# A transformer-mixer layer: memory queries and keys of all heads move into the seven-product stage

## The chip, the cores and the metric

The kernel runs on one core of a Trainium2 chip. The metric is device time in microseconds (us) of one execution, smaller is better. TensorE (PE) does the matrix products; VectorE (DVE) and ScalarE (ACT) read and write the tiles beside it; GpSimd (POOL) and SyncE (SP) mostly issue DMA transfers.

## The reference

One layer works on T = 640 tokens (512 latent, 128 context) of width 1024. Around it lie two half-step feed-forwards; between them stands the token mixer, which this change is about:

```
mq, mk, mv, mo, mg, dq, dk, dv, gm, gd = split_cols(h @ w_in)
dq, dk = rmsnorm(dq), rmsnorm(dk)            # 8 attention heads, 2 x 64 wide
q_att, keys = rope_2d(dq), rope_2d(dk)       # latent tokens only, + cached keys
s   = einsum('bqhcd,bkhcd->bhcqk', q_att, keys) * scale
pr  = softmax(s);  w = pr[:, :, 0] - lam * pr[:, :, 1]
att = rmsnorm(einsum('bhqk,bkhv->bqhv', w, vals)) * (1 - lam_init)
h_f = mlstm_chunkwise(mq / 16, mk, mv, log_i[0], log_f[0])   # 4 heads, 256 wide,
h_b = mlstm_chunkwise(reversed the same)                     # chunks of 128 tokens
hm  = rmsnorm(h_f + h_b) * sigmoid(mo)
y   = sigmoid(gm) * (hm @ w_br_m) + sigmoid(gd) * (att @ w_br_d)
out = y @ w_out
```

So ten projections of the same normalised activations h feed an attention branch and a memory branch (an mLSTM scan in both directions). mq, mk, mv, mo are 4 heads each; each head's 1024 x 256 block of weights is called a granule here, as is each quarter of the gates gm and gd and each pair of attention heads' dq, dk or dv. Nine vectors of modulation, products of a conditioning vector with columns of w_ada, scale, shift and gate the three parts.

## The kernel before, in words

Matrices are in float32, split into a high and a low part, and a product is three matmuls (high-high, high-low, low-high); a chunk of 128 of the inner dimension (8 chunks) thus gives 24 matmuls for one output tile, a *unit*. The mixer has four parts in time.

*The seven-product stage* (class `Gates`, a `Winograd`). For a granule whose output lies feature by feature, a 2 x 2 split of both operands needs 7 half-size products in place of 8: 7 x 4 x 3 = 84 matmuls of 128x320 (tile `ps_f`) rather than 96. VectorE and ScalarE make the sums of weights (`ww`, `wB`, `wC`) and combine the results, which go to DRAM (`g_out`, then `mq_dram`, `mk_dram`, `o_dram`, `gm_dram`, `gd_dram`). `self.work` is the list of granules in order: six of the gates, query and key of memory head 0, four of `mo`. A table `IN_GATES` places modulation tiles (class `Columns`, two VectorE passes `junk<-raw_a,csil` for each) at its granules.

*Attention.* Nine fill units, then eight heads. Each head has five slots, qi = 0 to 4, one for each 128 queries. A slot's scores (`sc`, 8 matmuls) are followed on VectorE by a reduce (`mn<-sc`, 1536 wide), on ScalarE by two exponentials (`p<-sc,mn`), on VectorE by `rc`, `r` and the mix `p`, on TensorE by the transposes `ps_wT` of slot qi, on ScalarE by the copies `wT`, and then by the values (`ps_o`). At the end of a head come its norm, the packing of the next head's queries and keys (`qT`, `kH`, `kL`) and the copy `aT`.

*The fill queue* (`fill`). Projections which are not due yet are units in one queue: token granules (`ps_t`, 5 units of 24 matmuls 128x256, results by token) and feature granules (`ps_p`, 4 units of 24 matmuls 128x320). The code calls `fill.units(n)` between the parts of a slot; the table `UNITS` tells how many stand at the two places of each slot of each head. A granule needs its weights loaded (`raw`), and split by ScalarE (`wH`) and VectorE (`wL`). A token granule of attention queries or keys is followed by norm and rope work on VectorE: `ss` (1280 wide), a scaling `*ry`, a multiplication by `g_kn` or `g_qn` and three passes 1024 wide with `ropeA` and `ropeB`.

*The memory scan* (class `Memory`). For each memory head, P (decays), va (values) and C (state) are loaded on SP's queue; ten cells (5 chunks x 2 directions) run; `fill.slot` places fill units there by a rate set with `fill.pace`. After the last cell the fill queue is drained, and the units of the next product follow (`w_brd`), interleaved with the last norm (`finish`).

Before the change queries and keys of memory heads 1 to 3 are feature granules of the fill queue; head 0's are read back from DRAM in attention head 1. Order on VectorE, ScalarE and TensorE is partly that of a scheduler and partly the order written out by hand (`with written()`).

Of the kernel before, what the change touches and what calls it, by code (L numbers as in the profile page):

```python
# [7 lines left out]
F32 = mybir.dt.float32  # L8
# [12 lines left out]
T = NS + NP  # L21
# [10 lines left out]
def tile_trunk(ctx: ExitStack, tc: tile.TileContext, a: dict):  # L32
# [1432 lines left out]
    def rope_place(of):  # L1465
        if not in_pools:
            return rope_p[0].tile([128, 5, 256], F32, tag="pk", name="rope", bufs=2)
        return pair(of, 2, "rope").rearrange("p a b -> p (a b)").rearrange("p (t n) -> p t n", t=5)

    at_rope = [None]  # L1470

# [24 lines left out]

    def project_q(pr, now=lambda f: f()):
        def make():
            q_tok[pr] = t = qk.tile([128, 5, 256], F32, tag="qtok", name="q_tok")

            def evac(p, i):
                act(t[:, i, :], p, AF.Copy)
                if i == 4:
                    now(lambda: qk_norm_rope(t, tabs[0]))

            return evac

        return a["w_dq"][pr], make

    def project_k(pr, now=lambda f: f()):  # L1510
        def make():
            if pr % 2:
                t = pair("k", 3, "k_tok").rearrange("p a b -> p (a b)").rearrange("p (t n) -> p t n", t=5)
            else:
                t = qk.tile([128, 5, 256], F32, tag="ktok", name="k_tok")
# [12 lines left out]

        return a["w_dk"][pr], make

    def project_v(pr):
        def make():
            v_tok[pr] = t = ap.tile([128, 7, 256], F32, tag="vtok", name="v_tok")
            nc.sync.dma_start(out=t[:, 4:6, :], in_=a["cache_v"][:, :, pr * 256 : (pr + 1) * 256])

            def evac(p, i):
                act(t[:, i if i < 4 else 6, :], p, AF.Copy)
                if i == 4:
                    nc.sync.dma_start(out=a["new_v"][:, pr * 256 : (pr + 1) * 256], in_=t[:, 6, :])

            return evac

        return a["w_dv"][pr], make
# [144 lines left out]
    def begin_pools():  # L1688
        gates.close()
        in_pools["k"] = ctx.enter_context(tc.tile_pool(name="mlk", bufs=1, side="right"))  # L1690
        in_pools["q"] = queries_of.enter_context(tc.tile_pool(name="mlq", bufs=1, side="right"))

    queries_of = ExitStack()

# [11 lines left out]

    mqT, mkT = {}, {}

    def q_evac(h):
        mqT[h] = pair("q", h, "mqT")  # L1710
        return lambda p, mt, hf: act(mqT[h][:, mt, half(hf)], p, AF.Copy, scale=0.0625)

    def load_memory(h):
        for box, tag, src in ((mqT, "q", mq_dram), (mkT, "k", mk_dram)):
            box[h] = pair(tag, h, f"m{tag}T")
            nc.sync.dma_start(out=box[h], in_=src[:, 2 * h : 2 * h + 2, :])

    def k_evac(h, by_act=False):
        mkT[h] = pair("k", h, "mkT")
        if by_act:  # L1720
            return lambda p, mt, hf: act(mkT[h][:, mt, half(hf)], p, AF.Copy)
        return lambda p, mt, hf: vec.tensor_copy(mkT[h][:, mt, half(hf)], p)

    def v_evac(h):
        def f(p, i):
# [12 lines left out]
    def values_of(h):  # L1738
        token((a["w_mv"][h], lambda: v_evac(h)))

    def queries_of_memory(h):
        feature(a["w_mq"][h], lambda: q_evac(h))

    def keys_of_memory(h, **kw):
        feature(a["w_mk"][h], lambda: k_evac(h, **kw))

    def projections(pr):
        token(project_k(pr))
        token(project_q(pr))
# [35 lines left out]
    class Gates(Winograd):  # L1785
# [3 lines left out]
        def __init__(self, fp, tmp, psum):  # L1789
            self.fp, self.tmp, self.psum = fp, tmp, psum  # L1790
            self.part = {(kh, hf): Of(kh, hf) for kh in range(2) for hf in range(2)}
            gate = [(a[n], dst, g, self.plain) for g in range(3) for n, dst in (("w_gd", gd_dram), ("w_gm", gm_dram))]
            rest = [(a["w_mq"], mq_dram, 0, self.query), (a["w_mk"], mk_dram, 0, self.plain)]
# [152 lines left out]
    def aside(hd, qi, part):  # L1946
# [8 lines left out]
        if part == 0 and hd == 1 and qi in (2, 3):  # L1955
            gate_cols()

    two, one = (1, 1), (1, 0)
    UNITS = {
        0: (two, two, two, two, one, (1, 1, 1)), 1: (two, two, two, one, one, (0,)),  # L1960
        2: (one,) * 5 + ((1, 1, 1),), 3: (two, one, one, one, one, (0,)),
        4: (one,) * 5 + ((1, 1, 1),), 5: (two, one, one, one, one, (1,)),
        6: (two, one, one, one, one, (1, 1, 1)), 7: (two, one, one, one, (0, 0), (0, 0)),
    }
    late = None
    for hd in range(8):
        H = heads[hd]
        odd = hd % 2
        for qi in range(5):
            n = UNITS[hd][qi]  # L1970
            with written():
                H.scores(qi)
                if qi > 0:
                    H.turn(qi - 1)
                H.soft(qi)
            aside(hd, qi, 0)
            fill.units(n[0])
            with written():
                H.mix(qi)
            if late is not None:  # L1980
                late()
                late = None
            if qi > 0:
                with written():
                    H.values(qi - 1)
            if qi == 3 and hd < 7:
                with written():
                    heads[hd + 1].pack()
            aside(hd, qi, 1)
            if (hd, qi) == (0, 2):  # L1990
                begin_pools()
            elif (hd, qi) == (1, 0):
                load_memory(0)
            fill.units(n[1])
            with written():
                fill.ahead()
        n = UNITS[hd][-1]
        with written():
            H.turn(4)
        if hd < 7:  # L2000
            N = heads[hd + 1]
            N.queries()
            fill.units(n[0])
            with written():
                H.values(4)
            H.finish_norm()
            if odd:
                for i in range(5):
                    fill.one()
                    if i in (0, 1):  # L2010
                        N.keys(i)
                    if i == 1:
                        with written():
                            fill.ahead()
            else:
                N.keys(0)
                fill.units(n[1])
                N.keys(1)
                with written():
                    fill.ahead()  # L2020
                fill.units(n[2])
# [174 lines left out]
    for h in range(4):  # L2196
# [372 lines left out]
```

## Time and profile before

| | us |
|---|---|
| median of 3 runs (lowest, highest) | 1813.63 (1813.38, 1814.05) |
| profiled execution | 1812.29 |
| its span, first to last instruction | 1810.5 |
| seven-product stage | 504.0 to 652.3 |
| attention, first fill units | 652.3 to 680.8 |
| attention, heads 0 to 7 | 680.8 to 1074.7 |
| memory scan and its drain | 1074.7 to about 1218 |

The profile gives each engine's busy time; since TensorE's matmul ends are modelled, the time from one issue to the next tells more than a busy share. "Idle before" names what ended an engine's wait. A chain of work, followed back from the last instruction, tells which engine the time belongs to. L75 is the line of the matmul helper, L51 that of ScalarE's helper, L54 and L57 those of VectorE's: groups are told apart by their tiles.

### The profile page before, as it was taken

How to read it: one execution, taken by the hardware profiler on the slowest of the kernel's cores; microseconds unless marked ns; L12 is line 12 of the kernel's file. 1: busy time of each engine (PE TensorE's matmuls, PEld its weight loads, DVE VectorE, ACT ScalarE, POOL GpSimd, SP SyncE). 2: the span in 40 equal slices, each digit the busy share in tenths (PEclk: the TensorE clock that was granted, in tenths of full speed). 3: DMA queues.
4: the chain of work that ended last, by engine and by line, in shares of the span. 5: the costliest groups of instructions: out<-in, count | busy, mean ns of one | idle time of the engine just before them, and what ended most of it. 6: DMA issues, size and time to landing. Idle time of an engine off the chain costs nothing.

```text
span 1810.5 us, 30758 instructions
## 1 busy us (share of the span) xinstructions
PE 1784.8 (99%) x12550; PEld 1743.7 (96%) x12550; DVE 1345.2 (74%) x2162; ACT 899.6 (50%) x1579; POOL 41.0 (2%) x72
## 2 busy tenths in 40 slices
PE   8999999999999999999999999999999999999998
PEld 7999999999999999999999998899999999999998
DVE  6889987677888765858585547877668888897485
ACT  5654544333655455656565546562326545554432
POOL 0000000100000000000000000000000000000010
PEclk9999999999999999999999999999999999999999
DMA  8355566977245544221221134565652455557992
GB/s 327 111 198 177 185 232 224 349 227 266 84 139 182 194 143 131 78 70 63 69 69 60 64 106 129 181 248 209 216 173 78 134 174 185 203 179 274 352 310 84
DMA packets 132207, 311.36 MB, mean 172 GB/s; under 512 B 10017, under 2 KB 93217, under 8 KB 119009
## 3 DMA queue, kind: packets, MB, share of 16 engines
q1 hardware_dynamic: 120690, 263.64, 42.2%
q0 software_dynamic: 10688, 43.13, 7.4%
q8 instruction: 98, 1.61, 0.4%
q10 hardware_dynamic: 688, 2.63, 0.4%
q14 instruction: 43, 0.35, 0.1%
HBM read 240.49 MB, written 68.87 MB: 171 GB/s over the span
## 4 chain that ended last, share of the span: by engine, by line
PE 83%; DVE 7%; DMA 5%; ACT 3%; issue 1%; SPq 0%; DVEq 0%; ACTq 0%
PE ps_f L75 49%; PE ps_p L75 13%; PE ps_t L75 12%; PE sc L75 2%; PE ps_o L75 2%; DVE ww L54 2%; DMA raw_a<-in_w_ada_k 1%; PE ps_qkT L78 1%; PE ps_wT L78 1%; DMA P<-nm_dram 1%; PE ps_n L75 1%; DMA raw<-in_w2b 1%; DVE junk L814 1%; PE ps_u L75 1%; DMA a_raw<-aT_dram 1%
## 5 line engine op out<-in xcount | busy, mean ns | idle before, releaser
L75 PE MATMUL ps_f<-S,ww 128*128 128x320 f32 x2400 | 387.1, 310 | 2.7 <-DMA S<-g_dram 0.9
L75 PEld LDWEIGHTS ps_f<-S,ww 128*128 128x128 f32 x2400 | 359.8, 188 | 6.7 <-DVE ww L54 4.6
L54 DVE TENSOR_TENSOR ww<-raw,ww 128x2048 fp32r<-128x2048 f32 (+1 forms) x73 | 163.9, 2245 | 65.9 <-ACT ww L51 65.8
L75 PE MATMUL ps_t<-wH,hH 128*128 128x256 f32 x640 | 185.1, 289 | 0.9 <-DVE x L57 0.9
L75 PE MATMUL ps_f<-hm,ww 128*128 128x320 f32 x1176 | 185.8, 309 | 0.1
L75 PE MATMUL ps_t<-wH,hL 128*128 128x256 f32 x640 | 181.0, 283 | 0.9 <-DVE hL L54 0.9
L75 PE MATMUL ps_t<-wL,hH 128*128 128x256 f32 x640 | 180.9, 283 | 0.0
L75 PEld LDWEIGHTS ps_f<-hm,ww 128*128 128x128 f32 x1176 | 175.7, 188 | 0.6 <-DVE ww L54 0.6
L51 ACT ACTIVATE ww<-raw 128x2048 fp32r<-128x2048 f32 (+1 forms) x73 | 136.8, 1874 | 58.8 <-DVE raw L54 34.9
L54 DVE TENSOR_TENSOR raw<-raw 128x1024 f32<-128x1024 f32 x186 | 160.8, 864 | 2.4
L75 PE MATMUL ps_f<-hm,wB 128*128 128x320 f32 x1008 | 161.5, 309 | 0.0
L75 PE MATMUL ps_p<-hH,wH 128*128 128x320 f32 x480 | 151.1, 315 | 0.7 <-ACT aT L51 0.7
L75 PEld LDWEIGHTS ps_f<-hm,wB 128*128 128x128 f32 x1008 | 151.3, 188 | 0.0
L75 PE MATMUL ps_p<-hH,wL 128*128 128x320 f32 x480 | 148.3, 309 | 0.0
L75 PE MATMUL ps_p<-hL,wH 128*128 128x320 f32 x480 | 148.3, 309 | 0.0
L51 ACT ACTIVATE u<-ps_f 128x320 f32<-128x320 f32 x129 | 55.8, 433 | 156.1 <-PE ps_f L75 155.9
L75 PEld LDWEIGHTS ps_t<-wH,hH 128*128 128x128 f32 x640 | 122.3, 191 | 1.5 <-ACT nsq L51 1.1
L75 PEld LDWEIGHTS ps_t<-wH,hL 128*128 128x128 f32 x640 | 122.4, 191 | 1.1 <-DVE hL L54 1.1
L75 PEld LDWEIGHTS ps_t<-wL,hH 128*128 128x128 f32 x640 | 122.5, 191 | 0.3
L1619 DVE TENSOR_REDUCE mn<-sc 128x2 f32<-128x1536 f32 (+1 forms) x40 | 59.5, 1488 | 56.0 <-PE sc L75 55.8
L54 DVE TENSOR_TENSOR wL<-raw,wH 128x2048 fp32r<-128x2048 f32 x37 | 84.6, 2288 | 21.6 <-ACT wH L51 21.3
L51 ACT ACTIVATE wH<-raw 128x2048 fp32r<-128x2048 f32 (+1 forms) x45 | 75.4, 1681 | 47.0 <-PE ps_p L75 35.3
(307 smaller groups left out, 3598.9 us busy)
## 6 DMA issues: line engine op xcount, KB each, us to landing
g_dram<-g SPq DMA_DIRECT2D x44, 640.0 KB, 7.5
raw_a<-in_w_ada_c POOLq DMA_DIRECT2D x38, 512.0 KB, 4.8
g_dram<-g SPq DMA_DIRECT2D x24, 480.0 KB, 8.2
raw<-in_w1b SPq DMA_DIRECT2D x11, 1024.0 KB, 4.8
raw<-in_w3b SPq DMA_DIRECT2D x11, 1024.0 KB, 6.4
raw<-in_w1a SPq DMA_DIRECT2D x10, 1024.0 KB, 4.8
raw<-in_w3a SPq DMA_DIRECT2D x10, 1024.0 KB, 6.2
hm<-g_dram SPq DMA_DIRECT2D x7, 1280.0 KB, 11.7
```

The costliest lines, as they stand in the source:

```text
L51: return placed(nc.scalar.activation(*args, **kw))
L54: return placed(eng.tensor_tensor(out=out, in0=in0, in1=in1, op=op))
L75: tc.keep_in_program_order(nc.tensor.matmul(*args, **kw))
L78: tc.keep_in_program_order(nc.tensor.transpose(*args, **kw))
L814: placed(vec.tensor_tensor_reduce(out=junk, in0=raw, in1=self.csil[:, v, :], op0=ALU.mult, op1=ALU.add, scale=1.0, scalar=0.0, accum_out=m ...
L1619: placed(vec.tensor_reduce(out=mn, in_=sv, axis=AX.X, op=ALU.min))
```

## The change

The queries and keys of memory heads 1 to 3, six granules, are taken from the fill queue and added to `Gates`, whose list has 18 granules now in place of 12. All `mq` and `mk` go through DRAM: `load_keys` reads the keys back in attention head 6, `load_queries` the queries at the start of the memory scan, head 0's first in SP's queue, those of heads 1 to 3 behind csil. `IN_GATES` covers granules 5 to 16: twelve modulation tiles are made there, and the five that were made in the memory scan are gone. The remaining granules of the fill queue are dealt as v0, then key, query, value of pairs 1 to 3, then the memory values, then the last quarter of gm and gd. `UNITS` has one unit in each slot of every head. Token tiles of queries, keys and values are double-buffered, the rope scratch takes tiles of the key pool, the drain leaves two granules at the end of attention rather than three, and the rate of fill units in the scan is 0.6 rather than 0.8.

```diff
@@ rope_place, project_q, project_k, project_v
-        return pair(of, 2, "rope").rearrange("p a b -> p (a b)").rearrange("p (t n) -> p t n", t=5)
+        return pair("k", "qk".index(of), "rope").rearrange("p a b -> p (a b)").rearrange("p (t n) -> p t n", t=5)
...
-            q_tok[pr] = t = qk.tile([128, 5, 256], F32, tag="qtok", name="q_tok")
+            q_tok[pr] = t = (ap if pr % 2 else qk).tile([128, 5, 256], F32, tag="qtok", name="q_tok")
...
-            v_tok[pr] = t = ap.tile([128, 7, 256], F32, tag="vtok", name="v_tok")
+            v_tok[pr] = t = ap.tile([128, 7, 256], F32, tag="vtok", name="v_tok", bufs=2)
@@ loads of memory queries and keys
+    def load_queries(h):
         mqT[h] = pair("q", h, "mqT")
+        nc.sync.dma_start(out=mqT[h], in_=mq_dram[:, 2 * h : 2 * h + 2, :])
+
+    def load_keys(h):
         mkT[h] = pair("k", h, "mkT")
+        nc.sync.dma_start(out=mkT[h], in_=mk_dram[:, 2 * h : 2 * h + 2, :])
@@ the fill queue
     token(project_v(0))
-    values_of(0)
-    values_of(1)
-    projections(1)
-    queries_of_memory(1)
-    token(project_v(1))
-    projections(2)
-    keys_of_memory(1)
-    token(project_v(2))
-    projections(3)
-    values_of(2)
-    token(project_v(3))
-    values_of(3)
-    queries_of_memory(2)
-    keys_of_memory(2)
-    queries_of_memory(3)
-    keys_of_memory(3, by_act=True)
+    for pr in range(1, 4):
+        projections(pr)
+        token(project_v(pr))
+    for h in range(4):
+        values_of(h)
     gate_unit(a["w_gm"], gm_dram, 3, memory)
     gate_unit(a["w_gd"], gd_dram, 3, memory)
@@ class Gates
-            for src, dst, g, f in gate[:4] + o[:1] + rest[:1] + o[1:2] + rest[1:] + o[2:3] + gate[4:5] + o[3:] + gate[5:]:
+            for src, dst, g, f in gate[:5] + qk[:3] + o[:1] + qk[3:5] + o[1:2] + qk[5:7] + o[2:3] + qk[7:] + o[3:] + gate[5:]:
...
-    IN_GATES = [(i, 1) for i in range(5, 12)]
+    IN_GATES = [(i, 1) for i in range(5, 17)]
@@ attention
-    two, one = (1, 1), (1, 0)
-    UNITS = {
-        0: (two, two, two, two, one, (1, 1, 1)), 1: (two, two, two, one, one, (0,)),
-        2: (one,) * 5 + ((1, 1, 1),), 3: (two, one, one, one, one, (0,)),
-        4: (one,) * 5 + ((1, 1, 1),), 5: (two, one, one, one, one, (1,)),
-        6: (two, one, one, one, one, (1, 1, 1)), 7: (two, one, one, one, (0, 0), (0, 0)),
-    }
+    one = (1, 0)
+    UNITS = {hd: (one,) * 5 + ((1, 1, 1),) for hd in range(7)}
+    UNITS[5] = UNITS[6] = (one,) * 5 + ((1, 1, 0),)
+    UNITS[7] = (one,) * 4 + ((0, 0), (0, 0))
...
-            elif (hd, qi) == (1, 0):
-                load_memory(0)
+            elif hd == 6 and qi < 4:
+                load_keys(qi)
...
-            if odd:
-                for i in range(5):
-                    fill.one()
-                    if i in (0, 1):
-                        N.keys(i)
...
-            fill.drain(3)
+            fill.drain(2)
@@ the memory scan
+    in_pools["q"] = queries_of.enter_context(tc.tile_pool(name="mlq", bufs=1, side="right", reuse_waits="tile"))
+    load_queries(0)
...
-    fill.pace(0.8, 1)
+    fill.pace(0.6, 1)
...
-    columns.place(5, csil2, load_columns_raw, 1)
+    for h in range(1, 4):
+        load_queries(h)
...
-            if n in ((5,), (3, 7), (3, 7), ())[h]:
-                columns.tile(m.at_vec)
```

The order on VectorE at the start of attention head 4 before: the last norm step of head 3, then the reduces of the first two slots.

```order
L54 TENSOR_TENSOR ao<-ao,ry 128x640
L1619 TENSOR_REDUCE mn<-sc 128x2
L1633 RECIPROCAL rc<-sm 128x2
L57 SCALAR_TENSOR_TENSOR r<-sm,nlam,rc 128x1
L57 SCALAR_TENSOR_TENSOR p_9492<-p_9493,r,p_9492 128x768
L1619 TENSOR_REDUCE mn<-sc 128x2
```

And after, at the same place:

```order
L54 TENSOR_TENSOR ao<-ao,ry 128x640
L54 TENSOR_TENSOR wL<-raw,wH 128x2048
L1477 TENSOR_REDUCE ss<-rope 128x20
L1616 TENSOR_REDUCE mn<-sc 128x2
L63 TENSOR_SCALAR rv<-ss 128x20
L1630 RECIPROCAL rc<-sm 128x2
L57 SCALAR_TENSOR_TENSOR r<-sm,nlam,rc 128x1
L57 SCALAR_TENSOR_TENSOR rt<-ry 128x20
L57 SCALAR_TENSOR_TENSOR p_9909<-p_9910,r,p_9909 128x768
```

The split of a token granule's weights and the sum of squares of a key granule, with its small steps, now stand among head 4's first reduce and mix.

SP's queue at the start of the memory scan before (mask, then P, va and C of memory head 0, csil, then P and va of head 1):

```order
L97 DMA mask<-in_mask 128x256
L97 DMA P<-nm_dram 128x5x128 x2
L97 DMA va<-v_dram 128x5x256
L97 DMA C<-in_c_aug 128x516 x2
L97 DMA csil<-csil_dram 128x2048
L2054 DMA P<-nm_dram 128x5x128 x2
L2057 DMA va<-v_dram 128x5x256
```

And after:

```order
L1707 DMA mqT<-mq_dram 128x1280
L97 DMA mask<-in_mask 128x256
L97 DMA P<-nm_dram 128x5x128 x2
L97 DMA va<-v_dram 128x5x256
L97 DMA C<-in_c_aug 128x516 x2
L97 DMA csil<-csil_dram 128x2048
L1707 DMA mqT<-mq_dram 128x1280 x3
L1680 DMA gm_dram<-stage 128x320 x2
L2015 DMA P<-nm_dram 128x5x128 x2
L2018 DMA va<-v_dram 128x5x256
```

Head 0's queries stand ahead of mask and P, the other three and two gate tiles ahead of head 1's P.

VectorE behind the last cell of the scan before (the last `hs` of a chunk, the norm's small steps, the five normalised chunks, then a weight split):

```order
L57 SCALAR_TENSOR_TENSOR hs<-ps_n_13109,den,hs 128x256
L63 TENSOR_SCALAR rv<-hss 128x5
L57 SCALAR_TENSOR_TENSOR rt<-ry 128x5
L54 TENSOR_TENSOR rt<-rt,rv 128x5
L57 SCALAR_TENSOR_TENSOR ry<-rt,ry 128x5
L57 SCALAR_TENSOR_TENSOR hs<-hs,ry,g_mh 128x256 x5
L54 TENSOR_TENSOR wL<-raw,wH 128x2048
```

And after:

```order
L57 SCALAR_TENSOR_TENSOR hs<-ps_n_13237,den,hs 128x256
L54 TENSOR_TENSOR wL<-raw,wH 128x2048
L63 TENSOR_SCALAR rv<-hss 128x5
L57 SCALAR_TENSOR_TENSOR rt<-ry 128x5
L54 TENSOR_TENSOR rt<-rt,rv 128x5
L57 SCALAR_TENSOR_TENSOR ry<-rt,ry 128x5
L57 SCALAR_TENSOR_TENSOR hs<-hs,ry,g_mh 128x256 x5
```

The weight split has come ahead of the norm's steps.

More of the change, by code (lines that the diff above doesn't have):

```diff
@@ L1511, in make @@
         def make():
[L1512 to L1515, printed above, removed]
+            t = (ap if pr % 2 else qk).tile([128, 5, 256], F32, tag="ktok", name="k_tok")
             k_tok[pr] = t
@@ L1690, in begin_pools @@
         in_pools["k"] = ctx.enter_context(tc.tile_pool(name="mlk", bufs=1, side="right"))
-        in_pools["q"] = queries_of.enter_context(tc.tile_pool(name="mlq", bufs=1, side="right"))
     queries_of = ExitStack()
@@ L1707, in tile_trunk @@
     mqT, mkT = {}, {}
-    def q_evac(h):
+    def load_queries(h):
         mqT[h] = pair("q", h, "mqT")
[L1711 to L1718, printed above, removed]
+        nc.sync.dma_start(out=mqT[h], in_=mq_dram[:, 2 * h : 2 * h + 2, :])
+    def load_keys(h):
         mkT[h] = pair("k", h, "mkT")
-        if by_act:
-            return lambda p, mt, hf: act(mkT[h][:, mt, half(hf)], p, AF.Copy)
-        return lambda p, mt, hf: vec.tensor_copy(mkT[h][:, mt, half(hf)], p)
+        nc.sync.dma_start(out=mkT[h], in_=mk_dram[:, 2 * h : 2 * h + 2, :])
     def v_evac(h):
@@ L1739, in values_of @@
         token((a["w_mv"][h], lambda: v_evac(h)))
[L1741 to L1745, printed above, removed]
     def projections(pr):
@@ L1792, in __init__ @@
             gate = [(a[n], dst, g, self.plain) for g in range(3) for n, dst in (("w_gd", gd_dram), ("w_gm", gm_dram))]
-            rest = [(a["w_mq"], mq_dram, 0, self.query), (a["w_mk"], mk_dram, 0, self.plain)]
+            qk = [(a[n], dst, h, f) for h in range(4) for n, dst, f in (("w_mq", mq_dram, self.query), ("w_mk", mk_dram, self.plain))]
             o = [(a["w_mo"], o_dram, h, self.opening) for h in range(4)]
             self.work = []
-            for src, dst, g, f in gate[:4] + o[:1] + rest[:1] + o[1:2] + rest[1:] + o[2:3] + gate[4:5] + o[3:] + gate[5:]:
+            for src, dst, g, f in gate[:5] + qk[:3] + o[:1] + qk[3:5] + o[1:2] + qk[5:7] + o[2:3] + qk[7:] + o[3:] + gate[5:]:
                 gr = Granule(4, lambda raw, src=src[g]: dma(raw, src))
@@ L1967, in tile_trunk @@
         H = heads[hd]
-        odd = hd % 2
         for qi in range(5):
@@ L2006, in tile_trunk @@
             H.finish_norm()
-            if odd:
-                for i in range(5):
-                    fill.one()
-                    if i in (0, 1):
-                        N.keys(i)
[L2012 to L2021, printed above, removed]
+            N.keys(0)
+            fill.units(n[1])
+            N.keys(1)
+            with written():
+                fill.ahead()
+            fill.units(n[2])
             late = H.finish
```

## The prediction

> **What bounds the kernel now.** I read the page's busy shares first, then the 40 slices, then a table of windows by stage, and last the chain that ended last.
>
> ```profile
> PE 1784.8 (99%) x12550; PEld 1743.7 (96%) x12550; DVE 1345.2 (74%) x2162; ACT 899.6 (50%) x1579; POOL 41.0 (2%) x72
> ...
> PEclk9999999999999999999999999999999999999999
> ...
> PE 83%; DVE 7%; DMA 5%; ACT 3%; issue 1%; SPq 0%; DVEq 0%; ACTq 0%
> ```
>
> TensorE is busy at the full granted clock throughout, and 83% of the chain is its own. Matmul ends are modelled, so 99% hides short stalls; the windows, one for each stage that the change touches, show where they sit (columns: window, its length, then busy time and count of PE, PEld, DVE, ACT, POOL, the clock, DMA share, GB/s).
>
> ```profile
> 504.00:652.30 148.30, 148.30 (x1013) 148.30 (x1013) 116.52 (x154) 76.48 (x115) 3.71 (x7) 1.00 0.52 180
> 680.78:732.26 51.48, 51.48 (x432) 50.63 (x430) 29.90 (x48) 29.94 (x61) 0.00 (x0) 1.00 0.36 107
> 732.26:791.60 59.34, 58.98 (x471) 57.72 (x469) 41.47 (x65) 31.77 (x68) 0.00 (x0) 1.00 0.25 82
> 791.60:832.98 41.38, 41.04 (x341) 39.70 (x339) 27.71 (x44) 26.07 (x57) 0.00 (x0) 1.00 0.19 69
> 832.98:885.94 52.96, 52.15 (x413) 50.84 (x411) 39.48 (x61) 28.31 (x58) 0.00 (x0) 1.00 0.17 59
> 885.94:927.32 41.38, 41.04 (x341) 39.68 (x339) 27.71 (x44) 26.07 (x57) 0.00 (x0) 1.00 0.20 69
> 927.32:982.35 55.03, 52.77 (x436) 51.26 (x435) 37.88 (x57) 29.83 (x63) 0.00 (x0) 1.00 0.21 69
> 982.35:1029.05 46.70, 46.34 (x364) 45.18 (x363) 26.12 (x40) 25.55 (x55) 0.00 (x0) 1.00 0.22 76
> 1029.05:1074.65 45.60, 44.26 (x315) 42.74 (x313) 23.54 (x37) 20.60 (x43) 0.00 (x0) 1.00 0.12 43
> 1074.65:1207.00 132.35, 127.68 (x727) 113.65 (x727) 101.54 (x327) 79.50 (x216) 0.00 (x0) 1.00 0.54 171
> ```
>
> The first row is the seven-product stage, wholly TensorE-bound. Rows two to nine are the eight attention heads, 393.87 us together; the last is the memory scan, where 132.35 − 127.68 = 4.7 us are idle. In heads and scan, matmul units from the fill queue are what keeps TensorE busy while VectorE and ScalarE work. The next rows are the chain inside head 4 (start, length, what): a plain slot, then the first slots of head 5, which has work of rope on VectorE.
>
> ```profile
> 899.25 0.66 PE ps_wT L78 x6
> 899.91 2.88 PE ps_t L75 x24
> 902.78 1.34 PE ps_o L75 x12
> 904.12 1.40 PE sc L75 x8
> 905.52 0.66 PE ps_wT L78 x6
> ...
> 920.77 2.93 PE ps_t L75 x24
> ...
> 935.16 1.41 PE sc L75 x8
> 936.63 1.64 issue
> 938.27 2.28 DVE wL L54
> 940.55 1.40 DVE ss L1477
> ```
>
> A plain slot is 905.52 − 899.25 = 6.27 us with one token unit of 24 matmuls (2.88 alone, 2.93 beside others; I use 2.94 with the hand-over) in it. In head 5 the chain leaves TensorE for wL and ss on VectorE: the softmax waits behind them.
>
> **The change, part by part.** 1. Six granules (queries and keys of memory heads 1 to 3) join the seven-product stage, which goes from 12 to 18. One costs 148.30/12 = 12.36 us, so 6 × 12.36 = **+74.1**. The five added modulation tiles run on VectorE, priced by these groups (mean ns behind the busy time):
>
> ```profile
> L814 DVE CUSTOM_DVE_ANT_0 junk<-raw_a,csil 128x1024 bf16<-128x1024 f32 x14 | 17.1, 1218 | 0.3 <-DMA csil<-csil_dram 0.2
> ...
> L1619 DVE TENSOR_REDUCE mn<-sc 128x2 f32<-128x1536 f32 x32 | 56.2, 1756 | 54.0 <-PE sc L75 54.0
> L54 DVE TENSOR_TENSOR wL<-raw,wH 128x2048 fp32r<-128x2048 f32 x18 | 41.1, 2286 | 10.3 <-ACT wH L51 10.1
> L57 DVE SCALAR_TENSOR_TENSOR p<-p,r,p 128x768 f32<-128x768 f32 x32 | 32.6, 1018 | 1.0
> ...
> L1477 DVE TENSOR_REDUCE ss<-rope 128x20 f32<-128x1280 f32 x6 | 8.9, 1478 | 0.0
> ...
> L54 DVE TENSOR_TENSOR q_tok<-q_tok,ry 128x1280 f32<-128x1280 f32 x3 | 4.5, 1493 | 0.1
> ...
> L54 DVE TENSOR_TENSOR rope<-rope,ropeBk 128x1024 f32<-128x1024 f32 x3 | 3.7, 1217 | 0.0
> ...
> L51 ACT ACTIVATE p<-sc,mn 128x768 f32<-128x768 f32 x64 | 57.2, 901 | 24.8 <-DVE mn L1619 24.8
> ...
> L51 ACT ACTIVATE aT<-ps_aT,gs 128x512 f32<-128x512 f32 x8 | 5.5, 693 | 0.1
> ```
>
> A tile is two junk passes, 2.4 us. VectorE has (116.5 − 7 × 2.4)/12 = 8.3 us a granule, 10.7 with a tile: under 12.36, so the tiles cost nothing there; without that cover they would cost what exceeds 12.36. The added stores and weight loads find the DMA engines at 0.52 share.
>
> 2. Attention loses the twenty feature units (four in head 1, four in head 3, four in head 6, eight in head 7); its 81 units become 61, all token units, eight in heads 0 to 4 and seven in heads 5 to 7. Heads 2 and 4 of before have exactly the eight-unit pattern: 41.38 us, of which 41.38 − 8 × 2.94 = 17.86 is the head's own. All heads at that rate give 8 × 17.86 + 61 × 2.94 = 322.2, a gain of 71.7. But those two heads carry no rope work. The chain from a score to its transposed weights is reduce 1.76, two exponentials 1.9, reciprocal, ratio and mix 1.4, hand-overs 0.3: 5.4 of the 6.27 us of a slot. So 0.9 us of delay per slot is free, and the rest stops TensorE. A query or key granule brings wL 2.29, ss 1.48, the scale 1.49, three passes of 1.22: pieces longer than 0.9, in one strict order with the reduces. Before, heads 0, 1, 3 and 5 took this work under two units in their opening slots and, in the odd heads, five at the end. Now every slot has one. Head 5 before prices a granule met mostly with one unit: PE is idle 55.03 − 52.77 = 2.26, against 0.34 in head 4, so 1.9. The lower bound is 0 for a granule (hidden as in head 0), the upper 2.29 + 1.48 − 0.9 + 1.49 − 0.9 = 3.5. Walking the new order of ScalarE and VectorE with these durations I get 2.6, 2.8, 1.8 and 1.5 over the base in heads 0 to 3, nearest the 1.9.
>
> Head 4 is worse: wL and ss now stand in front of its first reduce (3.8 us), the 0.7 us aT copy stands between that reduce and the exponential, and the 1.49 us scale is ahead of the second reduce; with about 1.0 of smaller pieces, 7.0. Heads 5 to 7 do not meet rope: +0.5, +0.5, −0.4 by the walk. That makes 322.2 + 16.3 = 338.5, so **−55.4**; bounds −71.7 (all stalls hidden) and −39 (stalls twice as long).
>
> 3. The memory scan loses four feature units at 10.55/3 = 3.52 us (first row below): **−14.1**. But units are its cover. The rows are the chain, then ScalarE and VectorE at the end of the scan:
>
> ```profile
> 1207.31 10.55 PE ps_p L75 x72
> ...
> 1079.90 11.68 DMA P<-nm_dram
> ...
> 1111.91 5.69 DMA out_new_c<-Cn
> ...
> 1211.67 0.66 ACT L51 ACTIVATE Cn<-ps_u 128x258 f32<-128x258 f32 x2 [1.91 <-DMA out_new_c<-Cn]
> ...
> 1215.49 1.90 ACT L51 ACTIVATE wH<-raw 128x2048 fp32r<-128x2048 f32 x1
> ...
> 1212.70 0.17 DVE L57 SCALAR_TENSOR_TENSOR rt<-ry 128x5 f32<-128x5 f32 x1 [2.74 <-ACT ry L51]
> ...
> 1217.42 2.29 DVE L54 TENSOR_TENSOR wL<-raw,wH 128x2048 fp32r<-128x2048 f32 x1 [2.04 <-ACT wH L51]
> ```
>
> At the end, three units (10.55 us) cover the last norm, which closes at 1213.3, six us into them. Now one unit (3.52) is left, and wL (2.29) of a later granule is placed in front of the norm's last steps, with wH (1.90) on ScalarE. The norm then closes some 6 + 2.3 + 1 (half of wH) = 9.3 us in, 5.5 after the unit allowing 0.3: **+5.5**, between 0 (the split fits into the 2.74 us wait shown) and 9.3 − 3.5 + 1.9 = 7.7.
>
> At the start, the first memory queries (640 KB) go ahead of mask and P on SP's queue, and three more ahead of the next head's P, which already took 11.68 us of the chain. No transfer here shows them; by the stage's 171 GB/s one takes 3.8 us alone, but transfers overlap and three prefilled units of 3.5 cover most: +1.2 for the first, +0.5 for the second, between 0 and 3.8 + 2. The loads of keys, in head 6, see a DMA share of 0.22 and cost 0.
>
> Twelve us of modulation tiles leave VectorE here: −2, between 0 and the 4.7 idle. Three fewer units inside the cells leave the ScalarE–VectorE stretches of the chain (1111.9 onwards) less covered: +2, between 0 and 6. Together **+7.2**, between −5 and +16.
>
> 4. Double-buffered token tiles, a pool opened after attention and the moved rope scratch issue nothing new; their waits are on work that ends a head earlier, 0.
>
> Sum: 74.1 − 55.4 − 14.1 + 7.2 = **+11.8**. The profiled execution took 1812.29 (span 1810.5 and 1.79 around it), 1.34 under the median of 1813.63; so 1824.1 against it, **1825.4** as a median. A change under 0.2% (3.6 us) is about what cannot be told from none. Sorted otherwise: without new stalls the change is worth 74.1 − 71.7 − 14.1 = −11.7, and I expect S = 16.3 + 7.2 = 23.5 us of new stalls, because the units that left were cover.
>
> **Rivals.** *Cover holds (faster).* The time is then −11.7 + S with a small S. The place is heads 0 to 4: if VectorE does its rope pieces inside the 2.7 us that it idles in a plain slot (6.27 less reduce, mix and 0.8 of small pieces), S has only the scan's part or less. It decides at S = 11.7 − 3.6 = 8.1; with S = 3 as its middle, 1812.29 − 8.7 + 1.34 = 1804.9. For it speaks head 0 of before (PE 51.48 of 51.48 with rope work in it); against it head 5's 2.26.
>
> *A draw.* S between 8.1 and 15.3: 1810 to 1817. It needs, say, head 4 to cost 2 rather than 7 and the scan's end 1.5 rather than 5.5 (S = 14.5).
>
> *Transfers late at the scan's start, with the long bound in the heads.* +5 for queries and P, stalls in the heads half as long again (+8): S = 36.5, so 1838.4; before, P was waited for at 1079.90 in the chain, which speaks for it; the free 46% of DMA against.
>
> *The clock falls.* No stall of the chain above is over 1.64 us outside the scan's transfers, and the clock row is all nines; mine at the scan's end is 5.5. If half rate followed it, the next unit would take 7.0 instead of 3.5: 1828.9. [...]
>
> **How the numbers follow.** Forecast (1818 to 1832) 0.45; clock 0.10; late transfers 0.10; draw 0.19; cover holds 0.16. Slower by over 0.2% is the first three, 0.65; within 0.19; faster 0.16. Range 1809 to 1833: it takes in the draw and the edge of the faster case, and leaves out most of the faster one and the late transfers, 0.2 together. The forecast's own range is 1818 to 1832.
>
> **What would show it.** Seven-product stage 222 us, VectorE below it at about 178; more would say the tiles bound it. Heads 0 to 3 at 43 to 44, head 4 at 48, heads 5 to 7 at 38 to 39; head 4 at 42 and heads 0 to 3 at 41.5 would make the prediction wrong on the fast side. At the scan's end an idle TensorE of 4 to 7 us behind the norm, and no idle over 3 at its start.

## The result: 1829.1 us against 1813.5, slower by 0.9%

The median of 4 runs of the changed kernel is 1829.1 us (1827.8 to 1831.2); of 4 runs of the kernel before on the same chips 1813.51 (1812.36 to 1814.05). The ratio is 1.0088, with a 95% interval of 1.0070 to 1.0105: +15.6 us where +11.8 were forecast, inside the stated range. The profiled execution took 1828.8 us, with a span of 1827.0 (before 1810.5). Busy shares and chain of the changed kernel, from its page:

```profile
PE 1780.9 (97%) x12478; PEld 1736.3 (95%) x12478; DVE 1374.3 (75%) x2196; ACT 915.9 (50%) x1605; POOL 43.5 (2%) x77
...
PE 80%; DVE 10%; DMA 4%; ACT 4%; issue 2%; SPq 0%; DVEq 0%; ACTq 0%
```

TensorE is busy 3.9 us less than before (1784.8) although the span is 16.5 longer: its idle time has grown by 20.4 us, and VectorE's share of the chain has gone from 7% to 10%. What is new is waiting. The windows of the changed kernel, stage by stage (length, then busy time and count of PE, PEld, DVE, ACT, POOL, the clock, DMA share, GB/s): the seven-product stage, heads 0 to 7, the cells of the scan.

```profile
505.20:727.00 221.80, 221.80 (x1515) 221.80 (x1514) 171.86 (x221) 110.07 (x163) 6.34 (x12) 1.00 0.52 178
...
755.90:801.44 45.54, 41.02 (x336) 39.14 (x335) 36.21 (x57) 29.52 (x59) 0.00 (x0) 1.00 0.31 90
801.44:845.96 44.52, 42.20 (x351) 40.81 (x350) 30.87 (x55) 25.05 (x58) 0.00 (x0) 1.00 0.22 72
845.96:888.76 42.80, 41.04 (x340) 39.57 (x339) 34.28 (x54) 28.46 (x61) 0.00 (x0) 1.00 0.19 67
888.76:931.50 42.74, 41.15 (x340) 39.64 (x339) 30.30 (x47) 26.36 (x55) 0.00 (x0) 1.00 0.14 49
931.50:979.96 48.46, 43.22 (x340) 41.16 (x339) 37.99 (x60) 28.07 (x62) 0.00 (x0) 0.96 0.23 79
979.96:1018.34 38.38, 38.04 (x316) 36.70 (x315) 23.24 (x36) 23.27 (x50) 0.00 (x0) 1.00 0.22 74
1018.34:1059.13 40.79, 38.75 (x317) 36.79 (x316) 26.91 (x44) 23.12 (x55) 0.00 (x0) 1.00 0.27 90
1059.13:1098.46 39.33, 37.01 (x292) 34.74 (x291) 19.98 (x33) 20.07 (x48) 0.00 (x0) 1.00 0.18 59
...
1109.12:1220.64 111.52, 109.21 (x608) 96.15 (x606) 86.40 (x298) 72.31 (x203) 0.00 (x0) 1.00 0.51 164
```

| from the traces, us | before | after | change | forecast |
|---|---|---|---|---|
| up to the last product of the gate columns (same program) | 504.0 | 505.2 | +1.2 | 0 |
| seven-product stage and first fill units | 176.8 | 250.7 | +73.9 | +74.1 |
| heads 0 to 7 | 393.9 | 342.6 | −51.3 | −55.4 |
| start of the scan (three units) | 10.7 | 10.7 | 0.0 | +1.7 |
| cells of the scan, two units fewer | 121.6 | 111.5 | −10.1 | −7.0 |
| last cell to the last transposes, two units fewer | 25.8 | 27.8 | +2.0 | −1.6 |
| the rest (same program) | 577.8 | 578.6 | +0.8 | 0 |

The last two forecasts of the scan are the terms of the prediction sorted by place (each unit −3.5, the end +5.5, relief and lost cover in the cells 0). The end is where the largest single wait is. The chain of the changed kernel there, from the last weight split among the cells (start, length, what):

```profile
1215.63 2.29 DVE wL L54
1217.92 0.03 DVE num L54
1217.94 6.65 DMA raw<-in_w_brd
1224.62 1.92 ACT wH L51
1226.54 0.02 issue
1226.56 2.29 DVE wL L54
1228.86 0.09 DVE rv L63
...
1230.59 0.69 PE ps_hT L78 x2
1231.28 5.99 PE ps_p L75 x24
```

The norm's `rv` stands behind wL, wL behind wH, and wH behind a weight load that was issued only at 1217.9, by this chain when an earlier split was done with a buffer. The last unit also shows something else: 24 matmuls in 5.99 us where the next units of this chain take 3.52. The clock (third number from the end) in windows around head 4's idle stretch and around this one:

```profile
936.25:939.66 3.41, 0.87 (x6) 0.56 (x4) 0.62 (x4) 3.03 (x9) 0.00 (x0) 1.00 0.12 50
939.66:943.07 3.41, 3.41 (x16) 3.11 (x15) 3.34 (x5) 0.73 (x1) 0.00 (x0) 0.50 0.28 101
1224.40:1230.40 6.00, 0.13 (x1) 0.00 (x0) 3.22 (x6) 4.20 (x8) 0.00 (x0) 0.95 1.02 420
1230.60:1236.70 6.10, 6.10 (x24) 6.10 (x25) 2.02 (x5) 3.93 (x4) 0.00 (x0) 0.51 1.03 383
```

After TensorE had stood still, for 2.54 us in head 4 and 6.06 us here, the granted clock was 0.50: for 3.4 us in head 4 (939.66 to 943.07), for 6.8 us here (1229.79 to 1236.62).

### The profile page after: what moved, and what is told of

It is laid out like the page before. It is cut to its first block, busy times and chain, and to the rows that moved or that the text cites. A ratio compares the mean times of both kernels' runs of the same rounds, so it can differ in the third digit from the quotient of the medians.

```text
span 1827.0 us, 30766 instructions
## 1 busy us (share of the span) xinstructions
PE 1780.9 (97%) x12478; PEld 1736.3 (95%) x12478; DVE 1374.3 (75%) x2196; ACT 915.9 (50%) x1605; POOL 43.5 (2%) x77
## 3 DMA queue, kind: packets, MB, share of 16 engines
q1 hardware_dynamic: 124290, 268.89, 42.7%
## 4 chain that ended last, share of the span: by engine, by line
PE 80%; DVE 10%; DMA 4%; ACT 4%; issue 2%; SPq 0%; DVEq 0%; ACTq 0%
PE ps_f L75 51%; PE ps_p L75 10%; PE ps_t L75 8%; PE sc L75 2%; PE ps_n L75 2%; PE ps_o L75 2%; DVE ww L54 2%; DMA raw_a<-in_w_ada_k 1%; PE ps_wT L78 1%; DVE mn L1616 1%; PE ps_u L75 1%; ACT p L51 1%; DVE junk L814 1%; DMA raw<-in_w2b 1%; PE ps_qkT L78 1%
## 5 line engine op out<-in xcount | busy, mean ns | idle before, releaser
L75 PE MATMUL ps_f<-S,ww 128*128 128x320 f32 x2616 | 421.8, 310 | 3.5 <-ACT u L51 1.1
L75 PEld LDWEIGHTS ps_f<-S,ww 128*128 128x128 f32 x2616 | 392.2, 188 | 7.8 <-DVE ww L54 4.6
L54 DVE TENSOR_TENSOR ww<-raw,ww 128x2048 fp32r<-128x2048 f32 (+1 forms) x79 | 177.7, 2249 | 64.3 <-ACT ww L51 64.2
L54 DVE TENSOR_TENSOR raw<-raw 128x512 f32<-128x512 f32 (+1 forms) x204 | 176.8, 867 | 2.8
L814 DVE CUSTOM_DVE_ANT_0 junk<-raw_a,csil 128x1024 bf16<-128x1024 f32 (+1 forms) x86 | 104.8, 1219 | 4.0 <-DMA raw_a<-in_w_ada_c 3.4
L54 DVE TENSOR_TENSOR wB<-raw,wB 128x1024 fp32r<-128x1024 f32 x70 | 85.5, 1221 | 24.3 <-ACT wB L51 24.3
L51 ACT ACTIVATE wB<-raw 128x1024 fp32r<-128x1024 f32 x70 | 73.6, 1051 | 39.0 <-PE ps_f L75 14.6
L75 PE MATMUL ps_p<-hH,wH 128*128 128x320 f32 x288 | 90.0, 313 | 1.6 <-ACT aT L51 0.9
L75 PE MATMUL ps_p<-hH,wL 128*128 128x320 f32 x288 | 89.0, 309 | 0.0
L75 PE MATMUL ps_p<-hL,wH 128*128 128x320 f32 x288 | 89.0, 309 | 0.0
```

The costliest lines, as they stand in the source:

```text
L51: return placed(nc.scalar.activation(*args, **kw))
L54: return placed(eng.tensor_tensor(out=out, in0=in0, in1=in1, op=op))
L75: tc.keep_in_program_order(nc.tensor.matmul(*args, **kw))
L814: placed(vec.tensor_tensor_reduce(out=junk, in0=raw, in1=self.csil[:, v, :], op0=ALU.mult, op1=ALU.add, scale=1.0, scalar=0.0, accum_out=m ...
```

## The experiments

Heads with the same order repeat to 0.15 us or better from run to run where the clock does not change (head 3 takes 42.73 to 42.75 in five runs), so a single profile tells them apart. The cells are less sharp: in the nine runs without tiles there and with two units fewer than before they take 109.7 to 111.8 us. A single time is good to about 3 us only: 11 runs of one kernel (9, below) lay between 1811.9 and 1817.5. All edits are to the changed kernel unless said otherwise.

**1. The split of the next weights behind the norm.** `x_split_late`:

```diff
+            fill.eager = i > 0
+            if i == 1:
+                with tc.issue_after(mem[3].normed.ins), tc.issue_after(rstd_of.root.ins):
+                    fill.prefetch(1)
+                    fill.low()
             fill.one()
+            if i == 0:
+                fill.q[1][3] = load_raw(fill.q[1][0])
         mem[3].finish(i)
...
```

(`normed` and `root` are names given, in two lines left out here, to the norm's last step and its root.)

> One edit to the changed kernel: behind the last memory cell, the split of the next granule of w_brd (wH on ScalarE, wL on VectorE) is issued behind the norm's last steps instead of among them. Theory A (the 6.2 us of idle TensorE behind the scan come from wH, which waits for its weights until 1224.6 in ScalarE's queue, ahead of the last two squares): the norm closes at about 1226, the idle time falls from 6.2 to about 1.8 us, the clock is not reduced behind it, and the time falls by 7 us (4.4 of idle, 2.7 of clock), to about 1822. Rival (the idle time is the missing two units of cover, whatever the order): idle stays near 6, time unchanged within 1.5 us.

Measured: 1823.3 us. From the last cell to the last transposes 20.3 us instead of 27.8, −7.5. The windows from the last cell to the first transposes, and the next unit:

```profile
1223.24:1228.42 5.18, 3.89 (x27) 3.60 (x25) 2.15 (x10) 4.66 (x16) 0.00 (x0) 1.00 0.99 343
1228.42:1232.21 3.79, 3.79 (x27) 3.78 (x28) 3.73 (x5) 2.17 (x2) 0.00 (x0) 1.00 1.00 414
```

Idle 5.18 − 3.89 = 1.3 us, clock 1.00. Theory A holds: the order, not the missing units, made most of the gap. Before the change the split stood behind the norm on VectorE (wL at 1217.42, the norm's five steps from 1213.31), so the order is new and was not merely uncovered; why it came out so with two units fewer was not tested. What the missing units themselves cost here is at most the rest: 20.3 us against 25.8 − 7.0 = 18.8 before, 1.5 us.

**2. TensorE kept busy in the gap.** `x_clock`:

```diff
             fill.one()
+            if i == 0:
+                idle = psum.tile([128, 512], F32, tag="mm", name="ps_idle")
+                for _ in range(48):
+                    mm(idle[:, :128], identr, identr, start=True, stop=True)
```

> The changed kernel with 48 matmuls 128x128 on an identity, read by nobody, put in front of the last norm's transposes, so that TensorE works in the gap behind the scan. Theory B (the gap itself is 6.2 us, and the half clock behind it costs 2.7 us more by the 24 matmuls that took 6.17 instead of 3.52): about 4 to 5 us of the gap are filled, the clock row behind it stays at 1.00, the unit behind it takes 3.6, and the kernel is 2 to 3 us faster. Rival (the slow unit is slow for contention of DMA, 0.9 to 1.0 busy there, not for the clock): the unit still takes about 6, no gain.

Measured: 1827.12 us; the end took 25.1 us, −2.7. The instructions on TensorE in the gap, and the window of the unit behind it:

```profile
1226.04 5.47 PE L75 MATMUL ps_idle<-identr 128*128 128x128 f32 x48
1232.36 0.41 PE L78 MATMUL ps_hT<-ident,hs 128*128 128x128 f32 x2 [0.85 <-DVE hs L57]
```

```profile
1232.36:1236.13 3.77, 3.77 (x27) 3.76 (x28) 1.93 (x5) 2.94 (x4) 0.00 (x0) 1.00 1.02 419
782.91:786.32 3.41, 1.74 (x14) 1.34 (x13) 2.19 (x5) 3.41 (x8) 0.00 (x0) 1.00 0.00 0
786.32:789.73 3.41, 3.41 (x19) 3.41 (x18) 1.88 (x6) 1.57 (x7) 0.00 (x0) 0.50 0.00 0
```

Theory B holds: with DMA as busy as before (1.02), the unit takes its usual time. The half clock was 2.7 of the 9.0 us lost at the end. The transposes still come 10.0 us behind the last cell, as in the changed kernel, so the gap itself is unchanged and only the clock differs. The last two rows are from the same run's head 0: the clock also fell there, to 0.50, behind two idle stretches of only 0.90 and 0.77 us.

**3. The copy aT behind the exponentials.** `x_copy_late`: `with tc.issue_after(H.exp.ins): late()`.

> The changed kernel with the copy aT of the previous head issued behind the exponentials of a head's first slot; by the order this changes head 4 alone. Theory C (in head 4 the exponentials, ready at 935.4, wait in ScalarE's queue behind aT, which waits for TensorE until 936.4): they start about 1.5 us earlier, TensorE's idle stretch falls from 2.5 to 1, the clock is not reduced in head 4, and head 4 takes about 45 instead of 48.5 us. Rival (the reduce is late behind wL and ss, and that alone decides): head 4 stays at 47.5 or more.

Measured: 1826.62 us, but head 4 at 47.9 instead of 48.5; TensorE's idle stretch was 1.97, and the clock stayed at 1.00. Window of head 4, and its chain behind the exponentials:

```profile
932.45:980.39 47.94, 41.98 (x341) 39.76 (x340) 38.16 (x60) 28.18 (x62) 0.00 (x0) 1.00 0.23 79
```

```profile
941.23 1.49 DVE k_tok L54
942.73 1.67 DVE mn L1616
944.40 0.33 DVE k_tok L54
```

The rival holds: VectorE's own row sets head 4 (the scale k_tok before the reduce mn), so time gained on ScalarE returns only 0.5 us. A full clock alone returns nothing: in the run of experiment 2, with the order of the changed kernel, the clock did not fall in head 4, and it took 48.48 us.

**4. More cover in first slots.** `x_front`: `UNITS[hd] = ((1, 1),) + (one,) * 4 + ((1, 1, 0),)` for heads 0 to 4.

> The changed kernel with two units in the first slot of heads 0 to 4 and two instead of three at the head's end; the number of units in a head is the same. Theory D (stalls sit where the softmax chain is longer than one unit, and a second unit there covers them: 2.5 us in head 0, 1.6 in head 1, 2.7 and the clock in head 4): the five heads fall from 224.0 us by 4 to 7, head 4 to about 44. Rival (the third unit was needed at the head's end as much): 224 within 2 us.

Measured: 1834.91 us, the five heads 230.9 instead of 224.1. Head 0 fell to 42.9, but the windows of heads 2 to 4 say:

```profile
842.67:890.74 48.07, 43.16 (x340) 41.15 (x340) 37.61 (x55) 29.89 (x61) 0.00 (x0) 0.96 0.17 59
890.74:937.42 46.68, 42.62 (x341) 41.20 (x340) 25.40 (x41) 25.89 (x56) 0.00 (x0) 0.96 0.13 45
937.42:986.63 49.21, 43.73 (x340) 42.23 (x340) 38.97 (x62) 27.15 (x61) 0.00 (x0) 0.93 0.25 84
```

The chain at the start of head 3:

```profile
898.59 0.84 DVE ao L54
899.43 0.14 issue
899.56 0.74 PE ps_aT L78 x5
```

Theory D falls. The rival has the right reason, but not the size: it expected no change, and the heads lost 6.8 us. Without the third unit at the head's end, VectorE's row has the norm's last step `ao` behind the next head's first reduce and mix, at 898.6 (in the changed kernel it stands ahead of that reduce, at 889.7). The transposes ps_aT, which wait for `ao`, stand in TensorE's order between the two units of the first slot, so the second unit covers nothing: TensorE idled 3.7 us, and the clock fell in three heads (means 0.96, 0.96 and 0.93).

**5. No rope.** `x_no_rope` leaves `qk_norm_rope` out for pairs 1 to 3.

> The changed kernel without norm and rope of the query and key granules of pairs 1 to 3 (their VectorE and ScalarE work is left out, the units stay). Theory A (the rope pieces between reduce, exponentials and mix are what heads 0 to 4 lose): the five heads fall from 224.1 us to about 210 (five times 41.4, and 2.5 for the late first reduce of head 0); heads 5 to 7 stay at 38.4 and 40.8. Rival (one unit a slot is too little cover whatever VectorE does): 220 or more.

Measured: 1811.57 us, with that work missing. Windows of heads 0 to 4:

```profile
754.65:797.53 42.88, 40.47 (x336) 39.16 (x335) 29.36 (x49) 26.27 (x56) 0.00 (x0) 1.00 0.39 128
797.53:839.88 42.35, 42.01 (x350) 40.78 (x349) 24.52 (x43) 23.59 (x53) 0.00 (x0) 1.00 0.22 74
839.88:881.25 41.37, 41.03 (x341) 39.69 (x340) 26.07 (x40) 24.47 (x54) 0.00 (x0) 1.00 0.19 69
881.25:922.61 41.36, 41.02 (x340) 39.67 (x339) 25.34 (x40) 25.11 (x54) 0.00 (x0) 1.00 0.15 54
922.61:965.17 42.56, 41.21 (x340) 39.67 (x339) 24.98 (x40) 23.23 (x53) 0.00 (x0) 1.00 0.18 64
```

210.5 us instead of 224.1; heads 2 and 3 take the 41.4 of the plain heads of before, and heads 5 and 6 stay at 38.4 and 40.8. Norm and rope under one unit a slot thus cost 13.5 us, 2.3 a granule.

**6. Seven tiles in the seven-product stage, five in the scan.** `x_tiles` has `IN_GATES` up to granule 11 and the five `columns.tile` of the scan back.

> The changed kernel with seven modulation tiles in the seven-product stage and five in the memory scan, as before the change. Theory B (tiles are hidden in the seven-product stage, and cost VectorE time in the scan): the stage up to the first scores stays at 250.7 us within 0.3, the cells grow from 111.5 by 2 to 4. Rival (hidden in both places): cells stay within 1.

**7. The kernel before with all twelve tiles in its seven-product stage.** `x_before_tiles`, an edit to the kernel before:

```diff
-    IN_GATES = [(i, 1) for i in range(5, 12)]
+    IN_GATES = [(i, 1) for i in range(5, 12)] + [(i, 0) for i in range(7, 12)]
...
-    columns.place(5, csil2, load_columns_raw, 1)
...
-            if n in ((5,), (3, 7), (3, 7), ())[h]:
-                columns.tile(m.at_vec)
```

> The kernel before with one part of the change alone: all twelve modulation tiles in the seven-product stage (still 12 granules; five of them take two tiles), none in the memory scan. Theory B (five tiles cost the scan 5.9 us and the seven-product stage hides them): the stage up to the first scores grows by 0 to 3 us (a granule with two tiles has 13.1 us of VectorE work against 12.36), the cells fall from 121.6 to about 116, the kernel is 3 to 6 us faster than before. Rival (before the change, feature units in the scan already hide the tiles): no gain, within 1.5 us of before.

Measured: 6 took 1835.32 us, with its stage up to the first scores at 250.7 and its cells at 117.4, +5.9. 7 took 1816.77 (11 runs; before 1811.96 in 21; ratio 1.0022, interval 1.0013 to 1.0031), with 177.0 for the stage and 121.9 for the cells. The windows of the cells, of 6 and then of 7:

```profile
1111.12:1228.50 117.38, 109.86 (x608) 97.53 (x606) 96.30 (x319) 72.17 (x203) 0.00 (x0) 0.99 0.57 183
```

```profile
1088.77:1210.64 121.87, 117.72 (x655) 104.29 (x653) 87.88 (x299) 75.56 (x202) 0.00 (x0) 0.99 0.42 138
```

Tiles are hidden in the seven-product stage in both (+0.0 and +0.2 us), so that part of theory B holds. In the scan of the changed kernel they cost more than expected; up to 1.7 us of the 5.9 is one stretch of 3.4 us at half clock (mean of the row 0.99), behind an idle stretch of 4.1 us. In the scan of before, with seven units in the cells instead of five, taking work off VectorE (busy 97.5 us in the cells before, 87.9 now) gained nothing. The rival is right about the cells: a weight split came into the tiles' place in VectorE's row, and an idle stretch of 2.5 us with a clock of 0.5 behind it. But neither theory expected this kernel to be slower as a whole, by 0.13 to 0.31%. Two clock falls in the profiled run (one in the scan, one in head 5, which took 56.5 us instead of 55.0) can be part of it; the rest is open.

**8. Two rope passes on GpSimd.** `x_rope_pool`, with the edit of 1, takes `ropeB` and the last sum to `nc.gpsimd` (for five of the six granules; the first key granule stays on VectorE).

> The kernel with the late split behind the scan, and two of the three 1024-wide rope passes of each query and key granule on GpSimd, which is idle, rather than VectorE. Theory A (VectorE's pieces among the softmax are the cost): 2.4 us of VectorE less for each of five or six granules, heads 0 to 4 fall from 224.9 to about 217, the time to about 1815. Rival (the passes are slower there and the granule is late, or VectorE is slowed while GpSimd runs): no gain in the heads.

Measured: 1827.38 us, the five heads 232.9 (225.6 in run 1), head 4 at 52.1. Instructions of GpSimd, then of VectorE, in head 2 (start, length, what):

```profile
860.94 2.63 POOL L54 TENSOR_TENSOR rope<-rope,ropeBk 128x1024 f32<-128x1024 f32 x1 [47.61 <-ACT rope L51]
864.79 2.34 POOL L54 TENSOR_TENSOR k_tok<-k_tok,rope 128x1024 f32<-128x1024 f32 x1 [1.22 <-DVE rc L1631]
```

```profile
861.25 3.40 DVE L54 TENSOR_TENSOR k_tok<-k_tok,ropeAk 128x1024 f32<-128x1024 f32 x1
864.76 2.38 DVE L57 SCALAR_TENSOR_TENSOR r<-sm,nlam,rc 128x1 f32<-128x1 f32 x1
```

The rival holds: a pass takes 2.3 to 3.1 us there, and VectorE's instructions that met it took longer. Its pass with `ropeA` ends 1.1 us behind GpSimd's first pass and takes 3.40 us where 1.22 is usual; the tiny `r`, usually 0.22, ends together with GpSimd's second pass and takes 2.38. So VectorE's busy time in the five heads rose, from 170.0 us in run 1 to 174.7, although ten passes had left it.

**9. Two key granules back in the fill queue**, with the edit of 1: `x_keys_late` (keys of memory heads 2 and 3, ten units in heads 0 to 3, two tiles in the scan), then `x_keys_tiles` (the same, all tiles in the stage):

```diff
+    for hd in range(4):
+        UNITS[hd] = ((1, 1), one, (1, 1), one, one, (1, 1, 1))
...
+        if pr == 2:
+            keys_of_memory(3)
         token(project_v(pr))
+        if pr == 1:
+            keys_of_memory(2)
...
```

> The kernel with the late split behind the scan, and the keys of memory heads 2 and 3 back in the fill queue: 16 granules in the seven-product stage, two more units in each of heads 0 to 3, in their first and third slots; two modulation tiles go back to the scan. Pure work: two granules of 12.33 less, eight units of 3.59 more, +4.0 us. Theory C (units are cover where the softmax waits for rope): stalls fall by 5 to 8 us and the time is 1819 to 1822, against 1823.3. Rival (as two units in first slots did, the units only move the stalls): 1827 or more.

> As the run with the keys of heads 2 and 3 in the fill queue (16 granules, late split), but with all twelve modulation tiles in the seven-product stage. Theory B: the cells fall by 3 us from 114.1, to about 111, the rest as in that run, 1815 to 1817. Rival (the two tiles cost nothing in the scan): 1819 to 1820.

Measured: 1819.35, and 1815.53 (11 runs; before 1811.96; ratio 1.0020, interval 1.0011 to 1.0029). Windows of head 1 and of the cells of the first, then of the cells of the second:

```profile
782.02:832.04 50.02, 50.02 (x399) 49.15 (x397) 27.19 (x45) 26.33 (x56) 0.00 (x0) 1.00 0.23 76
...
1105.86:1219.92 114.06, 110.42 (x608) 96.29 (x605) 90.83 (x308) 73.58 (x209) 0.00 (x0) 1.00 0.54 180
```

```profile
1102.43:1212.85 110.42, 108.46 (x607) 96.71 (x606) 86.45 (x298) 73.06 (x205) 0.00 (x0) 1.00 0.52 168
```

The stage fell by 24.6 us. The five heads rose by 20.4 us for eight units worth 28.7, so stalls fell by 8.3 against run 1, or by 6.7 against the changed kernel itself, in whose head 0 the clock did not fall; in head 1 TensorE has no idle time left. Theory C holds. Without the two tiles the cells fell from 114.1 to 110.4, as theory B says.

**10. A third key granule, into head 4.** `x_four`: 15 granules in the stage, the keys of head 1 between key and query of pair 3, `UNITS[4] = ((1, 1),) * 4 + (one, (1, 1, 1))`, and the edit of 3.

> As the run with 16 granules, all tiles in the seven-product stage and the late split, but with the keys of memory head 1 in the fill queue as well (15 granules, stored to DRAM from there), between key and query of pair 3, four units more in head 4, two in each of its first four slots, and aT behind the exponentials. Pure work: 4 x 3.59 - 12.33 = +2.0 us. Theory C: head 4, 47.3 with 6 us of stalls, takes 55 to 57 with twelve units, stalls 1; the sum is 3 us faster, 1811 to 1814, level with before. Rival (stalls move on with the units): 1816 to 1819.

Measured: 1812.81 us (11 runs) against 1812.52 of before (15 runs), ratio 1.0000, interval 0.9991 to 1.0009. Windows of head 4 and of the cells:

```profile
917.50:973.65 56.15, 54.43 (x437) 53.18 (x435) 39.98 (x61) 30.98 (x67) 0.00 (x0) 1.00 0.29 98
...
1102.84:1213.29 110.45, 108.39 (x608) 96.55 (x606) 86.39 (x298) 72.10 (x201) 0.00 (x0) 1.00 0.49 165
```

Head 4 takes 56.2 us with twelve units, of which 54.4 are TensorE's. With half of the six granules moved, the twelve tiles in the stage, and the end put in order, the kernel is level with before. No version that does the whole work beats it.

## Why the prediction was right

*The stage.* +73.9 measured for +74.1; VectorE 171.9 of 221.8. Right, and the tiles cost nothing there (6, 7).

*Attention.* −51.3 for −55.4. Heads 1 to 4 came within 0.4 us of the walk (44.5, 42.8, 42.7, 48.5 for 44.2, 43.2, 42.9, 48.4); head 0 was 1.6 over it, head 6 1.9, head 7 1.3, head 5 0.6 under. That norm and rope among the softmax are the main cause is shown by experiment 5: 13.5 us go with them, where the walk had 15.7. But all new stalls in the heads are 20.4 us, not 16.3, and the 6.8 that are not rope were counted with 0.6. In head 0 they are 1.5 us: it takes 42.88 even without rope, since its first reduce comes only at 758.98, behind small steps of the memory's gates on VectorE. In head 6 two weight splits stand in front of a mix and idle TensorE for 0.6 and 1.0 us. In heads 1 and 4 about 1 us each stays without rope, so that they met the walk is in part luck. In head 4 the copy aT in front of the exponentials was counted with 0.7 us, and moving it gained 0.5.

*The scan's start.* +1.7 forecast, 0.0 measured: the three prefilled units take the same 10.7 us as before, so the longer queue costs nothing here.

*The cells.* Relief −2 and lost cover +2 were to cancel; they gave −3.1 beyond the two units. (The prediction speaks of three units fewer inside the cells; four units less the two at the end are two. And the bounds of its terms of the scan add up to +19.5, not +16.) The relief was put too small: with the tiles left in the scan, two units fewer cost 117.4 − (121.6 − 7.0) = 2.8 us (6), near the +2, and taking the five tiles away then gives 5.9 back (6; two give 3.6, 9). With seven units in the cells it gives nothing (7), so the two terms hang together. The cells of equal runs differ by up to 2 us, which is also the uncertainty of these figures.

*The scan's end.* +5.5 was forecast, 9.0 measured, and this is the term that was mis-sized most. Its step named wL and half of wH in front of the norm; in fact the whole of wH waited for its load until 1224.6, and wL behind it; 7.5 of the 9.0 us go when the split is moved (1), 2.7 of them the clock (2). The rival "the clock falls", given 0.10, thus came true together with the forecast, at 2.7 us instead of 3.5. The trace of before does not show the half rate that it takes: the clock row is all nines, and behind the kernel's first 60 us no idle stretch of TensorE there was over 1.5 us up to its last matmul. The runs showed it in the changed kernel: TensorE idled 6.06 us, and the unit behind took 5.99 us at a clock of 0.51, where 3.52 is usual.

By the spans (+16.5) the forecast of +11.8 was 4.7 short: 4.1 in the heads, 3.5 at the end and 2.0 in stages that no edit touches, less 1.7 at the start, 3.1 in the cells and 0.2 in the stage. So the mechanism was right, cover lost in the heads and at the scan's end against cheaper matmuls in the stage, and the total gained from misses that partly cancel: 7.6 us too little in the heads and at the end, 5.0 too much elsewhere. The clock rival's 1828.9 lies next to the measured 1829.1 by the same luck: its end is right, but it has the same misses elsewhere.

## What to carry to other kernels

A unit of matmul work that can be placed anywhere can be worth more than its matmuls: taking 24 units to a cheaper algorithm saved 0.5 us a unit here (11.7 us), and brought new stalls of about 1.1 a unit (26.2 us); eight units given back took away 8.3 us of stalls (9). Price a move of filler by walking the order of the other engines with their durations, slot by slot, and look for the work that will stand in front of a reduce or a norm once the filler is gone. Where filler ends, look first whether the prefetch of the next stage stands in front of the last dependent steps in the engines' order: moving it behind them gave back 7.5 us at that place.

## What the hardware showed that was not expected

The forecast counts with a full clock. The traces show 0.50 behind some idle stretches of TensorE, and not by their length alone. It followed 6.06 us at the scan's end and 4.1 us in the cells of experiment 6; behind 3.7 us in head 3 of experiment 4 the mean of 3 us (900.26 to 903.26) was 0.56. In head 4 an idle stretch of 2.54 us was followed by 0.50 in the changed kernel, but the same one in experiment 2 by 1.00; it lies in these two windows (1.23 and 1.31 us of it):

```profile
936.50:939.92 3.42, 2.19 (x19) 1.95 (x17) 1.31 (x2) 1.68 (x3) 0.00 (x0) 1.00 0.61 259
939.92:943.33 3.41, 2.10 (x13) 1.74 (x14) 2.02 (x7) 1.62 (x7) 0.00 (x0) 1.00 0.25 95
```

In head 0 a stretch of 2.36 us was followed by 1.00 in the changed kernel, one of 2.65 us by 0.50 in run 1, and in experiment 2 two of 0.90 and 0.77 us by 0.50. What decides between these cases was not shown. The price of a stall of 2 us thus differed from run to run. A fall cost 2.7 us at the scan's end (6.8 us at half clock) and 1.6 in head 0 (3.4 us; 47.1 instead of 45.5 in run 1), where TensorE was the limit, and nothing in head 4, where VectorE was. That this makes the times spread as they do (3.4 us in four runs of the changed kernel) is possible, but not shown: 21 runs of before spread over 6.3, and its profile has no fall but at the end.

In experiment 8 GpSimd and VectorE both had float32 passes 128x1024 with two operands. A VectorE pass that met one of GpSimd's took 1.93 to 3.42 us, one that met none 1.21 or 1.22. A reduce with one operand that met one took its usual 1.75 us.
